# Strip 3 of the last batch: two column groups go from VectorE's row reductions to TensorE's row-by-row matmuls (diagonal of a 2-D prefix sum, Trainium2)

## The chip, the core and the metric

One core of a Trainium2 chip runs the whole kernel; the other cores are idle. The metric is device time in microseconds (us) for one launch. The kernel before took 669.38 us, the median of three runs (668.57 to 670.83). A further execution was taken with the hardware profiler: 668.88 us, of which 667.2 us is the span from the first to the last instruction. Engines: PE is TensorE's matmul, PEld its weight load, DVE is VectorE, ACT is ScalarE, POOL is GpSimd, SP is SyncE.

## What is computed

```python
B, H, W = 4, 4224, 4224                       # x is (B, H, W) float32
ps = np.cumsum(np.cumsum(x, axis=1), axis=2)
diag = np.diagonal(ps, axis1=1, axis2=2)
return np.cumsum(diag, axis=1)                # (4, 4224)
```

For each matrix of the batch, the diagonal of the 2-D prefix sum is itself summed up along its length. Every element of x counts, so 4 x 4224 x 4224 floats must be read; the result is four rows of 4224 numbers.

## The kernel before

**Increments of the diagonal.** The step of the diagonal from index i-1 to i is the sum of row i left of and on the diagonal plus the sum of column i above it. The kernel therefore needs, for each i, a row sum over the lower triangle and a column sum over the upper one. Both are collected, for one batch, in one PSUM tile `d` of 11 rows by 384 columns: row k of `d` holds one *group* of 384 consecutive indices (`GW`, line 40). At the end of a batch a short chain (lines 467 to 494) adds the row sums in by matmuls, forms carries between groups, and scans `d` twice (line 487).

**Strips.** x is read as strips of 768 rows (`strip`, 128 partitions x 6 rows x 4224 columns), converted to bf16 on the way by GpSimd's DMA queue (`load_rows`, line 73). Three buffers rotate (`NBUF`, line 46), so each load is issued when the strip three places earlier has been used up. A batch has five such strips (s = 0 to 4) and half a strip of 384 rows. The last batch is cut differently: strips s = 0 to 3, then the six rows per partition of the next tile come as two halves of 384 rows each (lines 419 and 420; here *half 1* and *half 2*), and the last 384 rows, without what was loaded at the start, come in seven pieces (lines 439 to 457: `part_a` in two, `part_b` in five), so that little is left to do after the last byte.

**What is done with one strip** (`add_up`, line 342). Its own 768 columns on the diagonal, the block, are split by a mask into the upper part `mu` (line 353) and the rest (line 354), both on VectorE. To the right of the block lie whole groups whose column sums are wanted. There are two ways for a group:

- *row by row on TensorE* (lines 348 to 350): one matmul of 384 columns for each of the strip's six rows, straight from the strip, with a one-hot matrix `sel` that picks the row of `d`. These come first in TensorE's order and need nothing but the loaded strip.
- *by rows on VectorE* (`by_rows`, lines 356 to 362): one reduction adds the six rows of the group up to a 128 x 384 float32 tile `rowed`, and a single float32 matmul (line 368) brings it into `d`. The groups nearest the block are taken this way.

After that VectorE sums two of the six rows left of the diagonal (`acc`, line 372) and ScalarE the other four (line 371), in place. At the end of the strips VectorE copies `acc6` to `r6` (line 408), for which it needs the sums of both engines.

**The order is written by hand** (`tc.manual_schedule()`, line 61): each engine does its instructions in program order. In the last batch VectorE's order is: strip 3 (mask, subtract, `rowed` x3, `acc`), the copies of line 408, half 1 (mask, subtract, row sum), half 2 (mask, subtract, `parts`, and a reduction of `fold`), and the final chain. TensorE's order is: strip 3's matmuls, half 1's six matmuls from the strip and three from its `mu`, then 28 matmuls from constants whose result nobody reads (`ready`, lines 422 to 424), then twelve matmuls that fold 1920 columns of half 2 into `fold` (line 427), half 2's six matmuls, the row sums (lines 467 to 470), and the pieces of the last tile (`fold_a`, lines 471, 472, 483 and 519). GpSimd's order is the loads alone: half 1, half 2, then the seven pieces.

```python
ready = psum_s.tile([P, 512], FP32, name="fold")
for i in range(28):
    matmul(ready, ident_h, um6[:, i % F2, :512], start=True)
```

Of the kernel before, what the change touches and what calls it, by code (L numbers as in the profile page):

```python
# [17 lines left out]
def kernel(  # L18
# [22 lines left out]
    NG = N // GW  # L41
# [28 lines left out]
    def strip_tile():  # L70
        return strips.tile([P, F2, N], BF16, name="strip")

    def load_rows(o, b, r0):
        f = o.shape[1]
        nc.gpsimd.dma_start(  # L75
            out=o, in_=x[b, r0 : r0 + f * P, :].rearrange("(p f) w -> p f w", f=f)
        )
# [188 lines left out]
    def row_sums(acc, src):  # L266
        nc.vector.reduce_sum(out=acc, in_=src, axis=AX.X)  # L267
# [18 lines left out]
    def masked(o, i, m, acc):  # L286
        nc.vector.scalar_tensor_tensor(  # L287
            out=o,
            in0=i,
            scalar=1.0,  # L290
            in1=m,
            op0=ALU.mult,
            op1=ALU.mult,
            accum_out=acc,
        )
# [21 lines left out]
    for b in range(B):  # L317
        whole = b < LB
# [12 lines left out]
        def columns(j, lo, hi, rhs, same=False):  # L331


            k = row_of(j)
            lhsT = sel[:, NG - 1 - k : 2 * NG - 1 - k]
            if same:
                matmul_on(d[:, lo:hi], lhsT, rhs)
                return
            matmul(d[:, lo:hi], lhsT, rhs, start=first[0])
            first[0] = False  # L340

        def add_up(strip, f, r0, acc, um, fs=0, wp=0, ws=0, by_rows=0):


            nw = f * P // GW
            g = r0 // GW
            hi = r0 + f * P
            for j in range(g + nw + by_rows, NG):
                for q in range(f):
                    columns(j, 0, GW, strip[:, q, j * GW : (j + 1) * GW], q > 0)  # L350
            mu = mup.tile([P, f, f * P], BF16, name=f"mu{f}")
            block = strip[:, :, r0:hi]
            nc.vector.tensor_mul(out=mu, in0=block, in1=um)  # L353
            nc.vector.tensor_sub(out=block, in0=block, in1=mu)  # L354
            rowed = []
            for i in range(by_rows):
                rowed.append(mup.tile([P, GW], FP32, name=f"rowed{i}"))
                c0 = hi + i * GW
                row_sums(
                    rowed[i],  # L360
                    strip[:, :, c0 : c0 + GW].rearrange("p q c -> p c q"),
                )
            for h in range(nw):
                for q in range(f):
                    columns(g + h, 0, GW, mu[:, q, h * GW : (h + 1) * GW], q > 0)
            for i in range(by_rows):
                k = row_of(g + nw + i)
                matmul(d, sel_f[:, NG - 1 - k : 2 * NG - 1 - k], rowed[i])
            if fs:
                for q in range(fs):  # L370
                    act_sum(acc[:, q : q + 1], strip[:, q, :hi])
                row_sums(acc[:, fs:], strip[:, fs:, :hi])
            else:
                for q in range(f):
                    act_sum(acc[:, q, 0:1], strip[:, q, wp:ws])
                row_sums(acc[:, :, 1], strip[:, :, ws:hi])

        acc6 = smalls.tile([P, NS, F2], FP32, name="acc6")

        ns = NS if whole else NS - 1  # L380
        for s in range(ns):
            strip = prefetched.pop(0) if prefetched else None
            if strip is None:
                strip = strip_tile()
                load_rows(strip, b, s * F2 * P)
            add_up(
                strip,
                F2,
                s * F2 * P,
                acc6[:, s],  # L390
                um6,
                F2 - 2,
                by_rows=min(2 if s == 0 else 3, NG - 2 * s - 2),
            )
            if not whole and s == 0:
                diag_b = last.tile([P, P], BF16, name="diag_b")
                nc.gpsimd.dma_start(out=diag_b, in_=x[b, TB:N, TB:N])
            if not whole and s == 1:
                row_sums(hs[:, 2:3], diag_b)
                masked(hmu[:, 2, :P], diag_b, um1[:, :P], hu[:, 2:3])  # L400
                nc.vector.tensor_sub(out=dtot, in0=hs[:, 2:3], in1=hu[:, 2:3])
                for h in range(3):
                    columns(LG, h * P, GW, hmu[:, h, : GW - h * P], h > 0)
# [198 lines left out]
```

## Time and profile before

| | us |
|---|---|
| median of three runs | 669.38 |
| the three runs | 669.38, 670.83, 668.57 |
| the profiled execution, whole | 668.88 |
| its span | 667.2 |
| VectorE busy | 428.7 (64%) |
| TensorE matmuls busy | 222.5 (33%) |
| ScalarE busy | 193.2 (29%) |
| GpSimd busy | 31.7 (5%) |

The busy times are means over stages with different limits. In each strip VectorE works without a break from the moment the load lands until `acc` is done, and then waits for the next load; what a change in one strip is worth is read from what waits behind it there. The 1.7 us between the span and the execution's own time lie around the first and the last instruction. In the answers of the trace that are shown below, times are from the start of the span; a line of the timeline gives start, duration, engine, line, operation, output and input with their shapes, how many instructions are merged in it, and in square brackets the idle time before it with what ended it.

### The profile page before, as it was taken

Reading aid. Unit: us, or ns where it says so; the run is one execution under the profiler, and the core shown is the slowest. Engines: PE = TensorE matmul, PEld = TensorE weight load, DVE = VectorE, ACT = ScalarE, POOL = GpSimd, SP = SyncE. Lnnn points to the kernel's source line nnn. Section 1 sums busy time; section 2 is a strip of 40 time slices with the busy share of each in tenths; the row PEclk is TensorE's granted clock in tenths of the full one; section 3 lists DMA queues with packets and bytes.
Section 4 is the critical chain, followed back from the end, with each engine's and each line's share of the span. In section 5 each row is a group of like instructions: output and inputs, shape, how many; then the busy total and the mean of one; then the engine's idle time right before and its main releaser. Section 6 shows DMA issues by size and latency. Waiting matters only on the chain.

```text
span 667.2 us, 2307 instructions
## 1 busy us (share of the span) xinstructions
PE 222.5 (33%) x858; PEld 82.7 (12%) x858; DVE 428.7 (64%) x194; ACT 193.2 (29%) x184; POOL 31.7 (5%) x60
## 2 busy tenths in 40 slices
PE   0071522223107254221321533323122244241458
PEld 0030110001103011000110210100001122010024
DVE  4181939596728294967862738577696364766895
ACT  0020305143802031433570203224266021231543
POOL 5200000000000000000000000000000000001000
PEclk9995856555558575565555956656565576675559
DMA  9999999999999999999999999999999999999997
GB/s 203 219 219 219 218 219 219 219 219 217 210 211 216 219 219 216 219 219 219 218 219 218 216 217 209 216 219 217 217 216 219 222 217 217 217 211 216 220 208 140
DMA packets 7665, 143.22 MB, mean 215 GB/s; under 512 B 698, under 2 KB 998, under 8 KB 2150
## 3 DMA queue, kind: packets, MB, share of 16 engines
q0 software_dynamic: 7312, 142.47, 99.7%
q1 hardware_dynamic: 342, 0.61, 0.3%
q8 instruction: 6, 0.10, 0.1%
q14 instruction: 5, 0.04, 0.0%
HBM read 285.47 MB, written 0.07 MB: 428 GB/s over the span
## 4 chain that ended last, share of the span: by engine, by line
DVE 54%; another core or an unknown queue 27%; ACT 10%; DMA 5%; PE 3%; issue 1%; POOL 0%; DVEq 0%; ACTq 0%; POOLq 0%
DVE rowed L267 26%; DVE acc L267 10%; ACT strip L262 10%; DVE mu L353 8%; DVE strip L354 8%; DMA strip<-in_x_dram 5%; PE fold L218 1%; PE d L218 1%; DVE c L487 1%; DVE whole_sums L487 0%; PE fold L225 0%; DVE pu L267 0%; DVE whole_sums L287 0%; DVE rows L408 0%
## 5 line engine op out<-in xcount | busy, mean ns | idle before, releaser
L262 ACT ACTIVATE strip<-strip 128x768 bf16<-128x768 bf16 (+8 forms) x90 | 189.0, 2101 | 458.9 <-DVE strip L354 458.9
L267 DVE TENSOR_REDUCE rowed<-strip 128x384 f32<-128x2304 bf16 x47 | 189.2, 4078 | 0.0
L353 DVE TENSOR_TENSOR mu<-strip,um 128x4608 bf16<-128x4608 bf16 (+1 forms) x24 | 52.4, 2183 | 195.4 <-DMA strip<-in_x_dram 195.3
L225 PEld LDWEIGHTS <-sel 128*11 128x11 bf16 x468 | 50.7, 108 | 374.2 <-issue 357.0
L218 PE MATMUL d<-rowed,sel_f 128*11 128x384 f32 x94 | 57.3, 705 | 109.3 <-DVE rowed L267 109.3
L267 DVE TENSOR_REDUCE acc<-strip 128x2 f32<-128x1536 bf16 (+4 forms) x19 | 90.8, 4777 | 0.0
L218 PE MATMUL d<-strip,sel 128*11 128x384 bf16 x55 | 23.5, 428 | 167.3 <-DMA strip<-in_x_dram 167.3
L225 PE MATMUL d<-strip,sel 128*11 128x384 bf16 x266 | 73.5, 421 | 13.8 <-DMA strip<-in_x_dram 13.8
L218 PE MATMUL d<-mu,sel 128*11 128x384 bf16 x43 | 17.8, 414 | 130.1 <-DVE mu L353 130.1
L225 PE MATMUL d<-mu,sel 128*11 128x384 bf16 x200 | 53.9, 412 | 0.0
L354 DVE TENSOR_TENSOR strip<-strip,mu 128x4608 bf16<-128x4608 bf16 (+1 forms) x24 | 52.4, 2183 | 1.5
L75 POOL DMA_DIRECT2D strip<-in_x_dram x23 | 15.7, 684 | 545.2 <-DVE acc L267 382.6
L218 PEld LDWEIGHTS d<-rowed,sel_f 128*11 128x11 f32 x94 | 5.4, 95 | 147.0 <-DVE rowed L267 146.4
L267 DVE TENSOR_REDUCE rows<-strip 128x1 f32<-128x4224 bf16 (+1 forms) x4 | 17.4, 4352 | 0.1
L262 ACT ACTIVATION_READ_ACCUMULATOR strip<-strip 128x1 f32 x90 | 16.8, 187 | 0.0
L218 PEld LDWEIGHTS <-sel 128*11 128x11 bf16 x99 | 10.8, 109 | 26.1 <-issue 16.7
L267 DVE TENSOR_REDUCE pu<-d 11x1 f32<-11x384 f32 x4 | 2.2, 545 | 14.1 <-PE d L218 14.1
L218 PE MATMUL d<-ident,rows 128*11 128x128 f32 x24 | 5.7, 373 | 16.5 <-ACT strip L262 16.5
L218 PE MATMUL fold<-um,ident_h 128*128 128x512 bf16 x28 | 7.7, 443 | 0.0
L101 DVE MEMSET um<- 128x4608 bf16 (+1 forms) x2 | 4.9, 2458 | 1.1 <-issue 1.1
L102 POOL TENSOR_SCALAR_AFFINE_SELECT um<-um 128x4608 bf16<-128x4608 bf16 (+1 forms) x2 | 5.2, 2610 | 7.0 <-DVE um L101 7.0
L218 PE MATMUL d<-halves,rows 128*11 128x64 f32 x48 | 5.3, 289 | 0.0
(114 smaller groups left out, 70.4 us busy)
## 6 DMA issues: line engine op xcount, KB each, us to landing
strip<-in_x_dram POOLq DMA_DIRECT2D x18, 6336.0 KB, 69.1
strip<-in_x_dram POOLq DMA_DIRECT2D x7, 3168.0 KB, 52.1
strip<-in_x_dram POOLq DMA_DIRECT2D x1, 1080.0 KB, 42.2
strip<-in_x_dram POOLq DMA_DIRECT2D x1, 768.0 KB, 45.2
strip<-in_x_dram POOLq DMA_DIRECT2D x3, 256.0 KB, 46.4
head<-in_x_dram SPq DMA_DIRECT2D x1, 528.0 KB, 3.9
strip<-in_x_dram POOLq DMA_DIRECT2D x1, 192.0 KB, 43.2
strip<-in_x_dram POOLq DMA_DIRECT2D x1, 64.0 KB, 28.6
```

The costliest lines, as they stand in the source:

```text
L75: nc.gpsimd.dma_start(out=o, in_=x[b, r0 : r0 + f * P, :].rearrange("(p f) w -> p f w", f=f))
L101: nc.vector.memset(um, 1.0)
L102: nc.gpsimd.affine_select(out=um, in_=um, compare_op=ALU.is_gt, fill=0.0, base=0, pattern=[[-1, f], [1, f * P]], channel_multiplier=-f,)
L218: nc.tensor.matmul(o, lhsT=lhsT, rhs=rhs, start=start, stop=False, skip_group_check=True)
L225: te.add_instruction(mybir.InstMatmult(start_tensor_calc=False, stop_tensor_calc=False, tile_position=(0, 0), tile_size=(P, P if lhsT.shap ...
L262: nc.scalar.activation(out=dump[:, :w], in_=src, func=ACT.Copy, accum_out=acc)
L267: nc.vector.reduce_sum(out=acc, in_=src, axis=AX.X)
L353: nc.vector.tensor_mul(out=mu, in0=block, in1=um)
L354: nc.vector.tensor_sub(out=block, in0=block, in1=mu)
L487: nc.vector.tensor_tensor_scan(out=to, data0=ones_row, data1=src, initial=carry[:, i : i + 1], op0=ALU.mult, op1=ALU.add,)
```

## The change

The number of groups that VectorE takes by rows is written out for each strip. For whole batches and for strips 0 to 2 of the last batch the numbers are those of before. In strip 3 of the last batch (rows 2304 to 3071, own columns 2304 to 3071, with the groups 8, 9 and 10 to its right) the number falls from 3 to 1: VectorE reduces group 8 alone, and groups 9 and 10 are read by TensorE, twelve bf16 matmuls ahead of strip 3's `mu` matmuls.

```diff
         ns = NS if whole else NS - 1
+        by_rows = (2, 3, 3, 3, 1) if whole else (2, 3, 3, 1)
         for s in range(ns):
...
-                by_rows=min(2 if s == 0 else 3, NG - 2 * s - 2),
+                by_rows=by_rows[s],
```

On VectorE two reductions are gone; on TensorE two float32 matmuls (`rowed`) are gone and twelve bf16 matmuls are added, in another place. The instructions and the order of ScalarE, GpSimd and SyncE, the loads among them, are those of before.

## The prediction

> **What bounds the kernel now.** First the page's rows of the DMA engines over 40 slices of the span, and its queues:
>
> ```profile
> DMA  9999999999999999999999999999999999999997
> ...
> q0 software_dynamic: 7312, 142.47, 99.7%
> ```
>
> The 16 DMA engines are busy from the first slice to the last but one: reading x sets the pace, and only what lies behind the last transfers can move the end. So I read the end alone. Next the timeline of GpSimd, whose last load is the last piece, and the page's row of that issue (KB, median us to landing):
>
> ```profile
> 634.14 0.53 POOL L452 DMA_DIRECT2D strip<-in_x_dram  x1 [14.42 <-DMA strip<-in_x_dram]
> ```
> ```profile
> strip<-in_x_dram POOLq DMA_DIRECT2D x1, 64.0 KB, 28.6
> ```
>
> The last piece lands at 634.14 + 28.6 = 662.7. Then the timeline of VectorE, from strip 3 to the end:
>
> ```profile
> 618.99 2.56 DVE L353 TENSOR_TENSOR mu<-strip,um 128x4608 bf16<-128x4608 bf16 x1 [7.83 <-DMA strip<-in_x_dram]
> ...
> 624.13 12.09 DVE L267 TENSOR_REDUCE rowed<-strip 128x384 f32<-128x2304 bf16 x3
> 636.12 6.56 DVE L267 TENSOR_REDUCE acc<-strip 128x2 f32<-128x6144 bf16 x1
> 642.78 0.36 DVE L408 COPY rows<-acc 64x24 f32<-64x24 f32 x2
> 643.17 0.76 DVE L353 TENSOR_TENSOR mu<-strip,um 128x1152 bf16<-128x1152 bf16 x1
> ...
> 648.95 0.76 DVE L353 TENSOR_TENSOR mu<-strip,um 128x1152 bf16<-128x1152 bf16 x1 [0.44 <-DMA strip<-in_x_dram]
> ...
> 655.41 0.66 DVE L267 TENSOR_REDUCE parts<-fold 128x3 f32<-128x480 f32 x1 [2.62 <-PE fold L225]
> ...
> 664.36 0.28 DVE L276 SCALAR_TENSOR_TENSOR pair<-strip 128x128 f32<-128x128 bf16 x1
> ```
>
> The last row is the sum of the last piece: it starts 1.6 us after the piece has landed. So the end isn't set by the last transfer but by a chain of work. The chain of waits names it: strip 3's `rowed` and `acc` up to 642.7, the mask of half 1, then TensorE's `ready`, `fold`, `d`, `fold_a`, then the carries and the two scans. The row at 643.17 has no wait in front: half 1 had long landed (GpSimd's issue at 634.14 had been waiting for a landing, which in the order of the queue is half 1's). VectorE is late by strip 3. The row at 648.95 waited for the landing of half 2, so VectorE has caught up there; TensorE hasn't:
>
> ```profile
> 643.98 0.48 PE L218 MATMUL d<-mu,sel 128*11 128x384 bf16 x1 [4.34 <-DVE mu L353]
> ...
> 645.03 7.70 PE L218 MATMUL fold<-um,ident_h 128*128 128x512 bf16 x28
> 652.78 0.36 PE L218 MATMUL fold<-strip,ident_h 128*128 128x480 bf16 x1
> 652.99 2.39 PE L225 MATMUL fold<-strip,ident_h 128*128 128x480 bf16 x11
> ```
>
> The 28 `ready` matmuls stand behind half 1's `mu` and end at 652.78, 3.83 us after half 2 has landed. That is what the lateness of VectorE costs: at most 3.83 us.
>
> **Step 1, VectorE in strip 3.** Three `rowed` take 12.00 us on the chain, 4.00 each. Two go: 8.0 us, and `acc` ends at 634.7 in place of 642.7. One `rowed` stays, so TensorE keeps one of its three float32 matmuls.
>
> **Step 2, ScalarE becomes the later one.** The copies of line 408 need ScalarE's sums too. ScalarE's last of strip 3:
>
> ```profile
> 632.55 2.75 ACT L262 ACTIVATE strip<-strip 128x3072 bf16<-128x3072 bf16 x1
> 635.20 0.19 ACT L262 ACTIVATION_READ_ACCUMULATOR strip<-strip 128x1 f32 x1
> ```
>
> They end at 635.39, so the copies start at about 635.45: 7.3 us earlier, not 8.0. Queued behind them on VectorE is half 1's mask, which starts at 635.85 (half 1 is there by 634.1, so no new wait for data).
>
> **Step 3, TensorE in strip 3.** Twelve matmuls from the strip are added at 618.95. In strip 2 twelve of this kind at the lower clock take 3.8 us (589.07 to 592.86), so they end at 622.8; strip 3's `mu` matmuls, which started at 621.61, are pushed back by 1.2 us and end near 627. The cover is TensorE's idle time from there to the landing of half 1, 7 us less what the one `rowed` matmul needs (1.45). Cost nothing; without the cover it would be these 3.8 us. VectorE's `mul` and `sub` don't wait for TensorE's reads: in strip 2, `sub` starts at 591.78, before those matmuls are through. Nor do the reads slow VectorE: its three `rowed` took 12.04 beside them in strip 2 and 12.09 without them in strip 3.
>
> **Step 4, `ready`.** Half 1's six matmuls start with its landing (634.1), its `mu` ones with the mask at 636.6, and `ready` at about 637.8 (645.1 - 7.3). At its 7.65 us it ends by 645.5. Half 2 lands at 648.85 as before, since no issue of GpSimd hangs on strip 3 of this batch. So `fold` can start at 648.95: the 3.83 us are gone, and the landing of half 2 is what is late next.
>
> **Step 5, the clock.** The 28 `ready` matmuls leave the clock raised; now 3.4 us or more of idle time lie behind them. The table by stretches (TensorE's granted clock is the third value from the right):
>
> ```profile
> 538.00:542.00 4.00, 2.18 (x12) 0.81 (x10) 4.00 (x2) 0.00 (x0) 0.00 (x0) 1.00 1.03 222
> 542.00:546.00 4.00, 1.45 (x2) 0.25 (x3) 2.03 (x2) 0.00 (x0) 0.71 (x1) 0.53 0.97 209
> ...
> 640.00:644.00 4.00, 0.02 (x1) 0.02 (x1) 3.82 (x5) 0.00 (x0) 0.00 (x0) 0.50 0.97 209
> 644.00:648.00 4.00, 4.00 (x11) 1.25 (x11) 3.96 (x2) 3.11 (x3) 0.00 (x0) 0.50 0.82 176
> 648.00:652.00 4.00, 4.00 (x20) 1.87 (x19) 3.49 (x4) 4.00 (x4) 0.00 (x0) 0.99 1.03 207
> ```
>
> In strip 0 of this batch TensorE went idle at 540.2, and by 542.3 the clock was at half. So I take it that `fold` starts at half clock. Now the clock comes back some time c after a burst starts: from the clock's mean over such stretches, 2.8 us in strip 0 (529.26, mean 0.62 over 529 to 533), 4.1 after 643.98, and 5.9 at most (259.83, mean 0.58 over 259 to 267). At half clock matmuls take twice as long (`ready` 0.427 against 0.213 each, the 384-wide ones 0.31 against 0.16). From the start of `fold` to the end of `d` it is 652.78 to 657.77 = 4.99 us at full clock; with c at half clock, 4.99 + c/2. So `d` ends at 648.95 + 4.99 + c/2: 655.3 for c = 2.8, 656.1 for the middle (4.35), 656.9 for 5.9, in place of 657.77. The gain there is 2.4, 1.7 or 0.9 us.
>
> Beside it: ScalarE's three sums of half 2 need its landing alone and take 3.6 us, ending at 652.7 instead of 654.8; VectorE's `parts` end at 652.8 as before. Neither ends last.
>
> The Trainium skill ("TensorE: Matmul & The Clock Gate", Part 1: The HAM clock gate) says that one idle window of about 3.4 us puts the clock to half, and that the window runs freely. It speaks against this change, which opens such a gap; strip 0 agrees with the drop, though only 2.1 us of idle time lay before it there. An example in the same section has the clock drop only 5.2 us after the last matmul; by that `fold` would run at full clock, and the sum would be 3.83 before the next step's cap.
>
> **Step 6, the last transfers cap it.** The rest of the chain moves up with `d`, until a piece isn't there yet. Landings by issue time and time to landing: `part_a` 654.0 and 657.7, `part_b` 658.9, 660.2, 661.4, 662.4 and 662.7. The last sum now starts at 664.36; it can start at 662.74 + 0.09 (the chain's steps between a landing and VectorE) = 662.83, 1.5 us earlier, and from there to the last write nothing changes. The others fit under such a shift: `fold_a` needs its second piece at 660.03 - 1.5 = 658.5, the weighted `part_b` at 661.11 - 1.5 = 659.6.
>
> **Sum.** The gain is the smaller of 1.5 and 3.83 - c/2: 0.9 for the latest clock, 1.5 for c under 4.7. I take 1.4. The profiled execution's span goes from 667.2 to 665.8 and its 668.88 to 667.5. That execution lies 0.5 under the median of the runs shown; from the median it is 669.38 - 1.4 = 668.0, which I give.
>
> **The rivals.**
> - *The whole 3.83 us or more*, if the last pieces land earlier too. The DMA row for 647 to 648 has a dip (share 0.58), while TensorE, VectorE and ScalarE all read the strips; if that is a collision, spreading the work could win 0.4 us of transfer and lift the cap. Against it: the share also dips at 631 to 632 (0.83), with TensorE idle. Price: gain 2 to 3, 667.0. Chance 6%.
> - *Nothing*: a piece's landing is not what the row says, or the copies, or `r6`, cost what was won. For it: 0.3% of this time is 2.0 us, about what a measurement of this kernel can tell from no change, and the slack is only 1.5. Time 669.3. Chance 9%.
> - *Slower*: the clock stays at half. It decides at c = 7.7 (the clock still at half at 656.6): from there `d` is later than before. If it never rises, `d` ends 1.2 later, the first seven `fold_a` cost 1.8 more, the matmuls from `fin_a` on (662.87 to 664.94) up to 2 more: 4 us in all, 673. Against it: no stretch of the trace took more than 5.9. In favour: the chain pauses between `d` and the carries, where TensorE waits. Chance 4%.
> - *It doesn't do what it says*: excluded; the order of instructions shows two reductions fewer and twelve matmuls more at this place.
>
> **Numbers.** Forecast (gain 0.9 to 1.5) 81%, more 6%, nothing 9%, slower 4%. The runs before spread from 0.8 below to 1.5 above their median. Under the forecast, a median that is 2.0 us (0.3%) below 669.38 needs 0.5 to 1.1 of scatter: a fifth of its 81%, 16%, and with the first rival faster has 21%. Slower by 0.3%: 4%. Within: 75%. Range: 1.5 gain and 0.8 of spread at the bottom, 667.1, and a little for the first rival, 666.7; no gain and some spread at the top, 669.9.
>
> **What would show it.** In the profile after: two fewer `rowed`; the copies of line 408 at 635.4 after ScalarE (step 2); `ready` at 637 to 638 with idle behind it (4); `fold` at 648.95 at a granted clock of 0.5 (5); the last sum within 0.2 us of its landing (6); the span at 665.7 to 666.3. I am wrong if `fold` doesn't start with the landing of half 2, if the clock isn't back by 655, or if the last landing moves by more than 0.5 us.

## The result and the profile after

The changed kernel takes 667.52 us, the median of eight runs (667.03 to 667.81), against 669.28 us (668.57 to 670.83, eight runs) for the kernel before. The ratio is 0.9971 with a 95% interval of 0.9960 to 0.9981: 1.8 us or 0.3% faster. The profiled execution took 667.1 us with a span of 665.4 us, 1.8 less than before.

VectorE's timeline of the changed kernel, for the rows shown of before:

```profile
623.91 4.08 DVE L267 TENSOR_REDUCE rowed<-strip 128x384 f32<-128x2304 bf16 x1
627.91 6.55 DVE L267 TENSOR_REDUCE acc<-strip 128x2 f32<-128x6144 bf16 x1
635.21 0.36 DVE L409 COPY rows<-acc 64x24 f32<-64x24 f32 x2 [0.75 <-ACT strip L262]
635.60 0.76 DVE L353 TENSOR_TENSOR mu<-strip,um 128x1152 bf16<-128x1152 bf16 x1
...
648.80 0.76 DVE L353 TENSOR_TENSOR mu<-strip,um 128x1152 bf16<-128x1152 bf16 x1 [7.87 <-DMA strip<-in_x_dram]
...
652.69 0.66 DVE L267 TENSOR_REDUCE parts<-fold 128x3 f32<-128x480 f32 x1
...
662.62 0.29 DVE L276 SCALAR_TENSOR_TENSOR pair<-strip 128x128 f32<-128x128 bf16 x1
```

Eight microseconds of reductions are gone, and 7.57 of them arrive at the copies: the row at 635.21 has waited 0.75 us for ScalarE, which now is the later of the two. After half 1 VectorE idles for 7.87 us until half 2 lands. Of 7.57 us only 1.74 are left at the last sum (662.62 against 664.36). TensorE's timeline shows where the first part of them went (the last row shown is the last of the matmuls that write `d`):

```profile
637.46 7.29 PE L218 MATMUL fold<-um,ident_h 128*128 128x512 bf16 x28
648.75 0.38 PE L218 MATMUL fold<-strip,ident_h 128*128 128x480 bf16 x1 [4.01 <-DMA strip<-in_x_dram]
648.97 3.69 PE L225 MATMUL fold<-strip,ident_h 128*128 128x480 bf16 x11
...
654.57 0.82 PE L218 MATMUL d<-ident,rows 128*11 128x128 f32 x6
```

The same last row in the kernel before:

```profile
656.95 0.82 PE L218 MATMUL d<-ident,rows 128*11 128x128 f32 x6
```

`ready` ends at 644.75, and `fold` starts with the landing of half 2, 4.03 us earlier than before, but takes 3.91 us from its start to its end in place of 2.60. `d` is complete at 655.39 in place of 657.77: 2.38 us. The last part goes at the end. This is the chain of waits of the changed kernel (start, duration, what), from strip 3 to the last instruction on an engine:

```profile
618.97 43.28 DMA strip<-in_x_dram
662.25 0.02 issue
662.27 0.41 DVE pair L276 x2
662.68 0.04 issue
662.72 0.48 PE fin_e L218 x6
663.21 0.02 issue
663.23 0.18 DVE ye L571
```

The chain of the kernel before ran through `rowed`, `acc`, `ready`, `fold` and the scans. Here it is one step: the last piece but one, issued at 618.97, lands at 662.25 after 43.28 us in the queue, and only the sums of the two last pieces, the last matmuls and the write follow. The transfers now set the end. A part of the 1.8 us is not the change's: in this execution the stream of loads ran 0.21 us ahead. GpSimd's issue behind strip 3's landing starts at 618.97; in the profile before it is this row:

```profile
619.18 0.53 POOL L452 DMA_DIRECT2D strip<-in_x_dram  x1 [4.31 <-DMA strip<-in_x_dram]
```

The same 0.21 us is in each of the differences above. Without it, 7.36 us arrive at the copies, `fold` starts 3.82 us earlier, `d` is complete 2.17 us earlier, and the last sum starts 1.53 us earlier, which is what the cap left.

### The profile page after: what moved, and what is told of

Read it like the earlier page. It is cut to its first block, busy times and chain, and to the rows that moved or that the text cites. A ratio compares the mean times of both kernels' runs of the same rounds, so it can differ in the third digit from the quotient of the medians.

```text
span 665.4 us, 2321 instructions
## 1 busy us (share of the span) xinstructions
PE 222.4 (33%) x866; PEld 83.5 (13%) x866; DVE 421.0 (63%) x192; ACT 193.5 (29%) x184; POOL 31.7 (5%) x60
## 4 chain that ended last, share of the span: by engine, by line
DVE 50%; another core or an unknown queue 27%; DMA 11%; ACT 10%; issue 1%; PE 1%; POOL 1%; DVEq 0%; ACTq 0%; POOLq 0%
DVE rowed L267 25%; DMA strip<-in_x_dram 11%; ACT strip L262 10%; DVE acc L267 9%; DVE mu L353 7%; DVE strip L354 7%; PE d L218 0%; DVE c L488 0%; DVE whole_sums L488 0%; POOL strip L453 0%; DVE pu L267 0%; DVE whole_sums L287 0%; POOL strip L442 0%; DVE rows L409 0%
## 5 line engine op out<-in xcount | busy, mean ns | idle before, releaser
L267 DVE TENSOR_REDUCE rowed<-strip 128x384 f32<-128x2304 bf16 x45 | 181.3, 4079 | 0.0
L218 PE MATMUL d<-rowed,sel_f 128*11 128x384 f32 x90 | 55.0, 706 | 104.9 <-DVE rowed L267 104.9
L218 PE MATMUL d<-strip,sel 128*11 128x384 bf16 x57 | 24.7, 433 | 182.9 <-DMA strip<-in_x_dram 182.9
L225 PE MATMUL d<-strip,sel 128*11 128x384 bf16 x276 | 78.1, 430 | 13.9 <-DMA strip<-in_x_dram 13.9
L218 PE MATMUL d<-mu,sel 128*11 128x384 bf16 x43 | 17.2, 400 | 112.8 <-DVE mu L353 112.8
L225 PE MATMUL d<-mu,sel 128*11 128x384 bf16 x200 | 50.2, 389 | 0.0
## 6 DMA issues: line engine op xcount, KB each, us to landing
strip<-in_x_dram POOLq DMA_DIRECT2D x1, 64.0 KB, 28.7
```

The costliest lines, as they stand in the source:

```text
L218: nc.tensor.matmul(o, lhsT=lhsT, rhs=rhs, start=start, stop=False, skip_group_check=True)
L225: te.add_instruction(mybir.InstMatmult(start_tensor_calc=False, stop_tensor_calc=False, tile_position=(0, 0), tile_size=(P, P if lhsT.shap ...
```

## The experiments

Two theories are kept apart from the start. **L**, the prediction's: VectorE's lateness cost time only because it held `ready`, and so `fold`, back beyond the landing of half 2, and the last transfers cap what can be won. **V**: VectorE's reductions lay on the path as such, some 0.9 us each. **T** is a rival to L's second half: the last transfer set the end all along. All ratios are to the kernel before on the same chip, with 95% intervals.

**1. The kernel before without `ready`.** The 28 matmuls are left out; nobody reads their result, so the output is whole.

```diff
-            ready = psum_s.tile([P, 512], FP32, name="fold")
-            for i in range(28):
-                matmul(ready, ident_h, um6[:, i % F2, :512], start=True)
```

> The kernel before with the 28 constant matmuls (ready) left out; their result is read by nobody. Theory L (the change won because it let fold start when half 2 lands, and the last transfers cap the gain at 1.5 us): fold starts at 648.9 instead of 652.8, at half clock for all or most of it, and d ends 0.9 to 2.4 us earlier: 0.9 to 1.7 us faster than the kernel before, although VectorE does all its three reductions. Rival V (the time of VectorE's reductions itself was on the path to the end, some 0.9 us per reduction): no gain, within 0.3 us of the kernel before.

Measured: 667.44 us against 668.97, ratio 0.9977 (0.9966 to 0.9987), 1.5 us faster, with all three reductions in place. TensorE's timeline:

```profile
648.89 0.56 PE L218 MATMUL fold<-strip,ident_h 128*128 128x480 bf16 x1 [3.80 <-DMA strip<-in_x_dram]
649.24 4.60 PE L225 MATMUL fold<-strip,ident_h 128*128 128x480 bf16 x11
```

`fold` starts with the landing and runs wholly at half clock (the clock came back at 654.3, 5.4 us after its start), and `d` is still complete at 656.50, 1.3 us earlier than in the kernel before, just under the cap of 1.5. V is out: the same gain, within the noise, comes without touching VectorE.

**2. The changed kernel with `ready` made longer.**

```diff
-            for i in range(28):
+            for i in range(65):
```

> The changed kernel with 65 in place of 28 ready matmuls, so that TensorE is held until about 652.6 as in the kernel before: 637.5 + 7.3 + 37 x 0.213. Theory L: the gain is undone, within 0.4 us of the kernel before (1.4 to 1.8 slower than the changed one), with fold at full clock. Rival V: the gain stays, 1.8 us faster than the kernel before.

Measured: 669.71 us against 668.97, ratio 1.0006 (0.9996 to 1.0016): the gain is gone. The median lies 0.74 us above that of the kernel before, more than the 0.4 expected; the interval, from 0.3 us faster to 1.1 us slower, includes no difference. TensorE's timeline:

```profile
637.76 15.19 PE L218 MATMUL fold<-um,ident_h 128*128 128x512 bf16 x65
653.01 0.36 PE L218 MATMUL fold<-strip,ident_h 128*128 128x480 bf16 x1
```

`ready` ends at 653.0, near where it ended in the kernel before (652.7). VectorE was as early as in the changed kernel (its copies at 635.51), which was of no use.

**3. Two groups by rows instead of one.**

```diff
-        by_rows = (2, 3, 3, 3, 1) if whole else (2, 3, 3, 1)
+        by_rows = (2, 3, 3, 3, 1) if whole else (2, 3, 3, 2)
```

> The changed kernel with two groups by rows on VectorE in strip 3 of the last batch, one in three of the change undone. Theory L: the copies start near 638.6, ready ends near 648.5 and fold starts with the landing of half 2, now at full clock throughout; the last transfers cap it: 1.5 to 1.9 us faster than the kernel before, like the changed one. Rival V: half the gain, 0.9 us.

Measured: 667.60 us against 668.97, ratio 0.9979 (0.9970 to 0.9987), 1.4 us: 0.1 less than the expected range, but about as much as run 4 wins on the same chip (1.45), for half the edit. V's 0.9 us lies at the edge of the interval (0.9 to 2.0), so it is runs 1 and 2 that rule V out. The copies are at 639.10, and `ready` ends at 649.45, 0.2 to 0.3 us after half 2 has landed (the load stream ran 0.3 us later than in the profile before). `fold` starts at 649.51 and, at full clock, takes 2.6 us: `d` is complete at 654.8, earlier than in the changed kernel. That this brings no more is the cap: the piece `part_a` is waited for on TensorE, and the last sum starts as its piece lands (634.44 + 28.8 = 663.2, sum at 663.22):

```profile
658.00 0.38 PE L218 MATMUL fold_a<-strip,ident_h 128*128 128x512 bf16 x1 [0.98 <-DMA strip<-in_x_dram]
```

**4. No group by rows.** The same line with 0 in the last place.

> The changed kernel with no group by rows on VectorE in strip 3 of the last batch. Theory L: the copies still wait for ScalarE until 635.2, so everything behind stays: 1.5 to 1.9 us faster than the kernel before, like the changed one. Rival V: 2.7 us faster. A third case, TensorE becoming the bound with 18 added matmuls: less gain than the changed kernel.

Measured: 667.52 us against 668.97, ratio 0.9977 (0.9969 to 0.9986), 1.45 us faster: about the same as with one or two, and V's 2.7 us lies outside the interval (0.9 to 2.1). VectorE's copies:

```profile
635.49 0.36 DVE L409 COPY rows<-acc 64x24 f32<-64x24 f32 x2 [4.62 <-ACT strip L262]
```

They wait 4.62 us for ScalarE: taking more from VectorE buys nothing from there, and the 18 added matmuls cost nothing.

**5 and 6. Both kernels without the last three loads.** The sums of rows 4160 to 4223 left of the diagonal block are left out (their place is set to zero on GpSimd), so 512 KB less are moved at the end.

```diff
+            nc.gpsimd.memset(part_b[:, 2:4], 0.0)
             for sb, c0, c1 in (
                 (0, 0, CB),
                 (1, 0, CB),
-                (2, 0, CB),
-                (3, 0, bcut),
-                (3, bcut, CB),
             ):
```

> The kernel before without the last three loads (512 KB, 2.4 us of transfer at 215 GB/s): the columns left of the diagonal block in rows 4160 to 4223 are set to zero on GpSimd in place of being loaded, so their sums are left out of the result. Theory L: the end hangs on the chain through ready and fold, and the transfers have slack: within 0.4 us of the kernel before. Rival T (the last transfer sets the end in both kernels, and what the change won came from an earlier landing): 2 to 2.4 us faster than the kernel before.

> The changed kernel without the same three loads, the same sums left out. Theory L: the cap of the last transfers is gone and the whole gain of the chain shows, d having ended 2.4 us earlier: 2.2 to 2.6 us faster than the kernel before, 0.5 to 0.9 more than the changed one. If the cap were not there: 1.8, as the changed one. Rival T: 3.8 to 4.2.

Measured: the kernel before with the cut takes 669.06 us against 669.32, ratio 0.9998 (0.9989 to 1.0007): the transfers had slack, T is out. The changed kernel with the cut takes 666.86, ratio 0.9964 (0.9952 to 0.9977), 2.5 us faster than the kernel before and 0.7 faster than the changed one in the same session (run 8). Between the two kernels with the cut it is 2.2 us (669.06 against 666.86). That is the 2.2 us by which `d` is earlier when the lead of the loads is taken off: with the cap lifted the chain's whole gain shows. The chain of waits of the changed kernel with the cut is again one of work, not of loads:

```profile
649.23 3.50 PE fold L225 x11
...
657.71 1.01 DVE c L486
658.75 1.00 DVE last_sums L486
```

**7. The changed kernel with `ready` long enough to keep the clock up.** As experiment 2, with 46.

> The changed kernel with 46 ready matmuls in place of 28: 18 more at 0.213 us fill TensorE's idle time, until about 648.6. Theory L: fold starts with the landing of half 2 at full clock, d ends 1.3 to 1.7 us earlier than in the changed kernel (near 653.8), and the end doesn't move because the last transfers cap it: within 0.3 us of the changed kernel, 1.5 to 1.9 faster than the kernel before. If the chain and not the transfers set the end there: 1.3 or more faster than the changed one, 3 or more faster than the kernel before.

Measured: 667.47 us against 669.32, ratio 0.9978 (0.9968 to 0.9987); the changed kernel beside it (run 8) has 0.9976. The step inside came out otherwise than expected: the clock rose only at 642.4 (639.7 in the profile of the changed kernel), so `ready` ran at half clock for longer and ended at 650.1, 1.1 us after the landing (ScalarE's first sum of half 2 starts at 649.05). `fold`, at full clock, started at 650.20, and `d` was complete at 655.2, only 0.2 us earlier than in the profile of the changed kernel, where 1.3 to 1.7 were expected. Even that could not be used: TensorE waits 0.51 us for `part_a` ahead of 657.91. The verdict (no change) is that of L, but this run shows the cap less sharply than run 3 does.

**8. The changed kernel again**, on the chip of 5 to 7.

> The changed kernel beside the three others, on their chip, as the reference for the differences: 1.5 to 2.0 us faster than the kernel before.

Measured: 667.59 us against 669.32, ratio 0.9976 (0.9966 to 0.9986).

## Why the prediction was right, step by step

- **Step 1** (8.0 us off VectorE) held: one `rowed`, `acc` done at 634.5.
- **Step 2** (ScalarE becomes the later one, 7.3 us left) held: 7.57 us, 7.36 without the lead of the loads. Run 4 shows the limit itself.
- **Step 3** (twelve matmuls at no cost) held: they end at 622.7, and run 4's eighteen cost nothing either. Strip 3's `mu` matmuls end at 624.7, not near 627, because the clock rose to full at 622.6. One argument of this step was misread: in strip 2 the twelve matmuls are over at 593.1, before `rowed` starts at 594.26, so that row does not show `rowed` beside them. What ran beside them, in strip 2 and in the changed strip 3 alike, are the mask and the subtraction, at the same 2.56 us each as in strip 3 of the kernel before.
- **Step 4** (`fold` starts with the landing) held: 648.75. Runs 1 and 2 show that this start is the cause, from both sides.
- **Step 5** was off in its mechanism in this execution. It let `fold` start at half clock and the clock return 2.8 to 5.9 us later, 1.7 us of gain at `d` for the middle. The clock was in fact still full when `fold` started, so the sign that the prediction named, a granted clock of 0.5 there, did not come. It fell only at 649.91, 1.2 us into `fold`, then stayed at half for 3.4 us. The cost is half of that, 1.65 us (6.64 from the start of `fold` to the end of `d` against 4.99), and the gain at `d` is 2.38, or 2.17 without the lead of the loads, inside the stated 0.9 to 2.4. In run 8, another execution of the same kernel, it went as the prediction had it: the clock had fallen at 648.84, before `fold` started at 649.31, and was back at 652.25, 2.9 us after that start (the prediction's c). From the start of `fold` to the end of `d` it is 6.44 us there, and the step's 4.99 + c/2 gives 6.46; in run 1, with c = 5.4, it is 7.61 against 7.7. The term 4.99 + c/2 was sound, but the moment at which the clock falls changes from one execution to the next. The table by stretches of the changed kernel (the granted clock is the third value from the right):

```profile
646.00:648.00 2.00, 0.00 (x0) 0.00 (x0) 0.00 (x0) 0.00 (x0) 0.00 (x0) 1.00 0.64 134
...
649.00:650.00 1.00, 1.00 (x6) 0.46 (x5) 0.96 (x2) 1.00 (x3) 0.00 (x0) 0.95 1.06 216
650.00:651.00 1.00, 1.00 (x4) 0.46 (x3) 0.97 (x2) 1.00 (x2) 0.00 (x0) 0.50 1.06 216
...
653.00:654.00 1.00, 1.00 (x8) 0.50 (x6) 0.52 (x2) 0.00 (x0) 0.00 (x0) 0.84 1.07 210
```

  The rule of the Trainium skill that was weighed there ("TensorE: Matmul & The Clock Gate", Part 1: The HAM clock gate: half rate after an idle window of about 3.4 us) agrees with what was seen only if the window is not counted from the last matmul: the clock fell 5.2 us after it, like the 5.2 us in that section's example.
- **Step 6** (the last transfers cap the gain at 1.5 us) held, and it made the error of step 5 harmless, as 2.17 and the 1.7 of the middle both lie above it. The last piece lands at 662.62 (633.92 + 28.7), just as its sum starts; the last piece but one, which the chain of waits names, lands 0.37 us earlier, and its sums keep the engine until then. Runs 5 and 6 show the cap by lifting it: without the last loads the kernel before gains nothing, the changed one 0.7 us.
- **The sum**: 1.4 forecast, 1.8 measured (1.3 to 2.7 by the interval). The forecast lies in that interval. Of the 0.4 us between them, 0.1 is what the forecast took off the cap for a late clock. In the profiles another 0.2 is the lead of the loads, which puts the span at 665.4, below the 665.7 to 666.3 that the prediction named; whether the medians hold such a lead isn't known. The gain of the same kernel in run 8 is 1.7 us. The runs of the kernel before also spread more (668.57 to 670.83 in eight runs) than those of the changed kernel (667.03 to 667.81 in eight). The length of `ready` varies with the moment at which the clock rises (7.65 us on the chain in the profile before, 8.04 in run 5), and the changed kernel hides that behind the landing. This is argued and not shown: runs 2 and 5, where `fold` waits for `ready`, spread over 2.2 to 2.5 us, and runs 4, 6 and 8, where it waits for the landing, over 0.5 to 0.9, but run 1, without `ready`, spreads over 2.6.
- **The rivals.** More than the cap by fewer collisions: the dip in transfers before 648 is still there (share 0.64 from 646 to 648) with every engine idle, so no collision with their reads makes it. Nothing, and slower through a clock that stays down: neither came; in run 1, where `fold` met the half clock for longest, the clock was back 5.4 us after `fold`'s start, before the 7.7 at which it would have cost time.

## What to carry to other kernels

Follow time taken off an engine from one join to the next: 8.0 us became 7.4 at a join with another engine, 3.8 at a join with a load, 2.2 after a stretch at half clock and 1.5 at the last transfers (all without the lead of the loads; 1.4 to 1.8 in the medians of the runs that kept the loads). Matmuls that only warm the clock stand in program order like all others: when their start depends on a late engine, they are late work themselves, and leaving them out was worth about as much here as the whole change. Where a stream of loads fills the span, compare each load's landing with the start of its first reader: that slack, found before the change, was about the most that an edit could win here while it left the loads as they were (1.5 us), and lifting it (run 6) brought the 2.2 us of the chain.

## What the runs showed of the hardware that was not expected

TensorE's clock stayed at full rate for 4.4 to 5.2 us after the last `ready` matmul: last end and fall at 644.75 and 649.91 (changed kernel), 644.72 and 649.56 (run 4), 644.89 and 650.02 (run 6), 644.39 and 648.84 (run 8), while in strip 0 of the profile before it fell about 2 us after the last matmul of a dense burst. In all four executions it was back about 3.4 us after it fell.

The falls have an order of another kind. In the same four executions the clock had risen during `ready` at 639.67, 639.31, 639.78 and 638.60, and in strip 0 at 532.02, with the fall at 542.26: each fall comes 10.24 us after its rise, which is three times 3.41, the time that it then stayed down in the four. In strip 3 of the changed kernel the fall comes 6.83 us after its rise (622.60 to 629.43), twice 3.41. These times fit a clock that is set anew every 3.41 us at moments that do not follow the matmuls; that is inferred from six falls, and no run was made to test it.

The idle time ahead of `fold` was 4.0 to 4.9 us in the four, and `fold` met a full clock in three of them and a half one in run 8. A gap of this length should be priced by both.
